# Four cost terms in a list scheduler's model: the port that VectorE and GpSimd share, transfer arrivals, block-solve matmuls, tile-size stickiness

## The chip, the cores and the metric

The kernel runs on one core of one Trainium2 chip. The core has a matrix engine (TensorE, PE in the profile, with its weight loads as PEld), VectorE (DVE), ScalarE (ACT), GpSimd (POOL) and SyncE (SP), which here only issues transfers. Each engine executes its own list of instructions in order and waits for the others at semaphores. SBUF is the on-chip memory, PSUM holds TensorE's results. The metric is device time in microseconds of one launch, lower is better.

## What is computed

Two trunk layers (D = 1024) over 640 tokens, of which 128 are a prompt and 512 a sample that starts from cached states. Each layer projects its modulated, normalised input to four recurrent mixers, each run forward and backward over the tokens, and has a feed-forward of 4096:

```python
def mixing_block(u, lp, init, pos):
    pa, pb, pc, pd = split_cols((u @ lp['w_in']), GROUP_COLS)
    ...  # mLSTM from pa, gated DeltaNet from pb, retention from pc, RWKV-7 from pd
    y = jnp.concatenate([ya, yb, yc, yd], axis=2).reshape(bsz, t, D_MODEL)
    return y @ lp['w_out'], (c1, n1, m1, sb1, sc1, sd1)

def trunk_layer(h, mod, lp, init, pos):
    sh1, sc1, g1, sh2, sc2, g2 = jnp.split(mod, 6, axis=-1)
    y, states = mixing_block(layer_norm(h) * (1.0 + sc1) + sh1, lp, init, pos)
    h = layer_norm(DEEPNORM_ALPHA * h + g1 * y, lp['ln1_g'], lp['ln1_b'])
    u = layer_norm(h) * (1.0 + sc2) + sh2
    f = jnp.square(jax.nn.relu(u @ lp['w_ff1'])) @ lp['w_ff2']
    h = layer_norm(DEEPNORM_ALPHA * h + g2 * f, lp['ln2_g'], lp['ln2_b'])
    return h, states
```

Here `mod = silu(cond) @ w_mod[l] + b_mod[l]`. Outputs are both token groups and the prompt's final states.

## The kernel before

The program is written once as plain calls, but nothing is issued then. Every call on an engine goes through `Engine.__getattr__` to `Plan.record`, which makes a node with its operands, its predecessors and an estimated duration from `Plan.cost` (for TensorE from `pe_time` and `pe_parts`). About 17,250 nodes come about. `Plan.schedule` then plays a run with these estimates: whenever an engine is free in that play, it takes the ready node of highest priority (`nd.prio`: place in the program, plus a little for the length of what follows) whose tiles can be had. `emit` issues the nodes in the order of their planned starts, so each engine's list, and SyncE's queue of transfers, is what the play produced. A different estimate thus changes the order of the lists, and nothing of what is computed. All instructions carry line 691 in the profile, the call in `emit`; the names of their tiles tell them apart.

Four things in the play matter here. First, the engine of some operations is chosen in it: `copyA` may run on ScalarE or VectorE, `tt` on VectorE or GpSimd, and a node moves off its preferred engine when the other is better by more than a slack. Second, TensorE's `pe_queue` prefers nodes of the tile size that runs already (128x128, or the small tiles of the block solves), unless another's priority is higher by `HY`. Third, a transfer's end is played as the later of a fixed latency and of the queue's bandwidth. Fourth, VectorE and GpSimd are played as independent.

Names used below. Full-precision products are made of a high and a low half: `split` takes a raw weight `wr` of 128x1024, `wh` is its rounded copy (`copyA`) and `wl` the difference (`tt`, GpSimd preferred); features have `uh` and `ul`, made from `u`. `pj` is a projection to a mixer, `pgj` that of the gates, `pwo` the output projection, `pff` the feed-forward. The modulation is made in chunks of 512 columns (`mod_chunk`): four products `pmod` from weights `wr` of `w_mod`, a copy `msb` to SBUF, in the gate sections the bias row by a transfer from `b_mod` into `msb`, then `pmt`, a second copy, and `pmg`, which puts the result into `modT`. `put` transposes a normalised tile `xn` before `u` is taken from it. In RWKV-7, `cum` are running sums of the log decay, `alp` and `kap` scaled keys, `psc` the score product of them, `lv` the 32x32 products of the block solves. `wscr` is a scratch in DRAM by which the solves' blocks are rearranged, `gh` what comes back from it.

The stages by the trace: start 0 to 120, mixing of layer 0 to 700, output projection and layer norm to about 790, its feed-forward to 1200, layer norm to 1300, mixing of layer 1 to 1850, output projection to 1937, feed-forward to 2347, and the end.

Of the kernel before, what the change touches and what calls it, by code (L numbers as in the profile page):

```python
# [80 lines left out]
class View:  # L81
    def __init__(self, tile, ops, p, ix, reg=None):
        self.tile, self.ops, self.p, self.ix, self.reg = tile, ops, p, ix, reg
# [130 lines left out]
class Plan:  # L214
    def __init__(self):
        self.nodes, self.tiles = [], []
        self.HY = 4.0
        self.bias = 0.0
        self.fill = False
        self.open_group, self.group_node = False, None  # L220
# [7 lines left out]
    @staticmethod  # L228
    def pe_parts(m, a):
        n = Plan.free_size(a[0])  # L230
        w = a[1].shape[1]
        w = 32 if w <= 32 else 64 if w <= 64 else 128
        if m == "transpose":
            return (n / 1200 + 0.0025,)
        if a[2].tile.dt == F32R:
            return (n / 2400 + 0.0135,)
        return (max(w / 1200, 2 * n / 2400) + 0.005,) * 2

    @staticmethod
    def pe_time(mem):  # L240
        t, end, pos = 0.0, 0.0, {}
        for m, fn, a, k in mem:
            p = (a[1].p[0], a[0].p[0])
            for d in Plan.pe_parts(m, a):
                t = max(t, pos.get(p, 0.0))
                pos[p] = t + d
                end = max(end, t + d)
                t += 0.0065
        return end
# [94 lines left out]
    def cost(self, nd, m, out, ins):  # L344
        e = nd.eng
        if e == "SP":
            o = nd.k["out"]
            i = nd.k["in_"]
            v = o if isinstance(o, View) else i
            n = 1  # L350
            for s in v.shape:
                n *= s
            return n * 4
        n = self.free_size(out)
        psum = any(v.tile.kind == "psum" for v in ins + [out])
        cols = sum(1 for v in ins if v.shape[-1] == 1 and n > 1)
        if e == "PE":
            return self.pe_time([(m, None, nd.a, nd.k)])
        if e == "DVE":
            if m in ("bn_stats", "reciprocal"):  # L360
                n = self.free_size(ins[0])
            if m == "bn_aggr":
                return 0.075
            if m in ("bn_stats", "transpose", "tensor_tensor_scan", "copy_predicated", "select", "tensor_tensor", "scalar_tensor_tensor") or psum:
                return n / 960 + 0.069 + (0.06 * cols if m != "tensor_scalar" else 0.0)
            return n / (1920 if m == "tensor_copy" else 1600) + 0.069 + 0.06 * max(0, cols - 1)
        if e == "ACT":
            return n / 1200 + (0.052 if psum else 0.094) + 0.093 * cols
        if e == "POOL":
            if m == "memset":  # L370
                return n / 1200 + 0.035
            if nd.k.get("op") == ALU.pow:
                return 0.165 * n + 0.3
            if m == "tensor_tensor":
                return n * 0.0021 + 0.148
            return n * 0.00333 + 0.176
        raise ValueError(e)
# [5 lines left out]
    def lat(self, a, b):  # L383
        if a == "SP":
            return 0.2 + SPM
        return self.LAT.get((a, b), 0.25)

    SPI = 0.48
    DLAT = 2.2
    DBW = 345.0*1e3  # L390

    def schedule(self):
        N = self.nodes
# [5 lines left out]
        for nd in reversed(N):  # L399
            d = nd.dur if nd.eng != "SP" else self.DLAT + nd.dur / self.DBW  # L400
            nd.cp = d + (max((self.lat(nd.eng, s.eng) + s.cp for s in nd.succs), default=0.0))
# [35 lines left out]
        for k, l in order.items():  # L437
            l.sort(key=lambda t: t.seq)
        nexti = dict.fromkeys(order, 0)
        for k, l in load.items():  # L440
            if l.max() > caps[k]:
                raise RuntimeError(f"{k} needs {l.max()} of {caps[k]}")
# [12 lines left out]
        free = {e: 0.0 for e in engs}  # L455
# [5 lines left out]
        dma_free = 0.0  # L461
# [3 lines left out]
        now = 0.0  # L465
# [89 lines left out]
        while True:  # L555
            progress = True
            while progress:
                progress = False
                for e in engs:
# [13 lines left out]
                    while h or e == "PE":  # L573
# [3 lines left out]
                        _, _, nd = heapq.heappop(q)  # L577
# [17 lines left out]
                        if b is not None:  # L595
                            wait[nd.idx] = nd
                            if b[0] == "g":
                                p = b[1]
# [19 lines left out]
                        if e == "PE":  # L618
                            cur = nd.grp
                            d = nd.dur + (SW if nd.mode != mode else 0.0)  # L620
                            mode = nd.mode
                            d *= 1 if warm else 2
                            hist.append((now, now + d, nd.act))
                            recent += nd.act
                            t0 = now
                            while t0 < now + d - 1e-9:
                                k = int(t0 / TICK + 1e-9)
                                t1 = min(now + d, (k + 1) * TICK)
                                cols[k] = cols.get(k, 0.0) + nd.act * (t1 - t0) / d
                                t0 = t1  # L630
                            nd.end = free[e] = now + d
                        elif e == "SP":
                            s = max(dma_free, now + 0.9)
                            dma_free = s + nd.dur / self.DBW
                            nd.end = max(now + self.DLAT, dma_free + 0.8)
                            free[e] = now + self.SPI
                        else:
                            nd.end = now + nd.dur
                            free[e] = nd.end
                        out.append(nd)  # L640
                        done += 1
# [24 lines left out]
            now = max(now, ev[0][0])  # L666
            while ev and ev[0][0] <= now + 1e-9:
                _, _, k, x = heapq.heappop(ev)
# [10 lines left out]
        if done != len(N):  # L679
            nd = N[floor]  # L680
# [1730 lines left out]
```

## Time and profile before

| | us |
|---|---|
| median of 3 runs | 2410.84 (2407.18 to 2411.10) |
| the profiled execution | 2401.18 |
| its span | 2399.5 |
| TensorE busy | 2125.6 (89%) |
| VectorE busy | 1536.5 (64%) |
| ScalarE busy | 937.9 (39%) |
| GpSimd busy | 702.4 (29%) |

The mean granted clock of TensorE was 0.929 in the profiled execution. A stage is read by setting the busy time of an engine against the stage's length; what ended an idle time is in the timeline's brackets.

### The profile page before, as it was taken

The page shows a single profiled execution, that of the slowest core. Times are in us where ns is not written, and L with a number is a line of the kernel's source. Part 1 is how long each engine was busy: PE and PEld are TensorE (multiplying, and loading weights), DVE is VectorE, ACT ScalarE, POOL GpSimd, SP SyncE. Part 2 cuts the span into 40 slices and gives each one's busy share as a digit, 9 for nine tenths or more (in the row PEclk, how much of TensorE's full clock was granted, in tenths as well). Part 3 has the DMA queues.
Part 4 walks back from the last instruction along what each step waited for, and adds up shares of the span by engine and source line. Part 5 has one row for each costly group of instructions (what it writes and reads, how often), then busy time and mean ns, then how long its engine had stood idle before and what let it go on. Part 6 is the DMA issues. An engine that isn't in the chain of part 4 may idle for free.

```text
span 2399.5 us, 42207 instructions
## 1 busy us (share of the span) xinstructions
PE 2125.6 (89%) x16510; PEld 1873.6 (78%) x16510; DVE 1536.5 (64%) x3349; ACT 937.9 (39%) x1979; POOL 702.4 (29%) x631
## 2 busy tenths in 40 slices
PE   5898798888887999999977898998988799999996
PEld 2787777687765988898866887888877689999994
DVE  5653965858679556655777758668976843333357
ACT  3332434333335544443334343343432443333332
POOL 2220512424047333333344313224423610000023
PEclk8978989899997999999998899899998899999998
DMA  8122324343644444444532121224245412222242
GB/s 262 28 65 74 81 82 132 76 118 87 207 141 150 126 124 138 140 132 123 177 107 63 36 68 36 64 75 102 82 127 168 140 62 79 71 79 78 72 158 88
DMA packets 317451, 253.13 MB, mean 105 GB/s; under 512 B 91100, under 2 KB 240828, under 8 KB 317252
## 3 DMA queue, kind: packets, MB, share of 16 engines
q1 hardware_dynamic: 317252, 250.43, 36.0%
q8 instruction: 130, 2.13, 0.4%
q14 instruction: 69, 0.57, 0.1%
HBM read 226.14 MB, written 24.24 MB: 104 GB/s over the span
## 4 chain that ended last, share of the span: by engine, by line
PE 32%; DVE 14%; issue 3%; DMA 2%; POOL 2%; ACT 1%; SPq 1%; POOLq 0%; ACTq 0%; DVEq 0%
PE pj L691 16%; PE pff L691 10%; DVE xn L691 2%; PE lv L691 1%; DVE cv L691 1%; DMA wr<-in_w_mod 1%; DVE acc L691 1%; DVE lnst L691 1%; DVE wl L691 1%; DVE osum L691 1%; PE poo L691 1%; SPq L691 1%; PE pwo L691 1%; DVE ew L691 0%; DVE fft L691 0%
## 5 line engine op out<-in xcount | busy, mean ns | idle before, releaser
L691 ACT CAST wh<-wr 128x1024 fp32r<-128x1024 f32 x228 | 238.8, 1048 | 453.4 <-PE pff L691 203.5
L691 PE MATMUL pff<-wh,hid 128*128 128x512 f32 x1280 | 403.2, 394 | 0.0
L691 PE MATMUL pj<-uh,wh 128*128 128x384 f32 (+1 forms) x1056 | 350.1, 332 | 9.3 <-ACT wh L691 8.5
L691 DVE TENSOR_TENSOR wl<-wr,wh 128x1024 fp32r<-128x1024 f32 x159 | 209.6, 1318 | 227.5 <-ACT wh L691 227.1
L691 PE MATMUL pj<-uh,wl 128*128 128x384 f32 (+1 forms) x1056 | 345.9, 329 | 9.2 <-POOL wl L691 5.3
L691 PE MATMUL pj<-ul,wh 128*128 128x384 f32 (+1 forms) x1056 | 343.8, 326 | 0.4 <-DVE ul L691 0.4
L691 PE MATMUL pj<-vh,wl 128*128 128x256 f32 (+1 forms) x1024 | 321.4, 314 | 6.5 <-POOL wl L691 5.5
L691 PE MATMUL pj<-vl,wh 128*128 128x256 f32 (+1 forms) x1024 | 320.9, 313 | 0.7 <-DVE vl L691 0.7
L691 PE MATMUL pj<-vh,wh 128*128 128x256 f32 (+1 forms) x1024 | 321.1, 314 | 0.3 <-ACT wh L691 0.3
L691 POOL TENSOR_TENSOR wl<-wr,wh 128x1024 fp32r<-128x1024 f32 x75 | 187.9, 2506 | 422.6 <-ACT wh L691 332.8
L691 PEld LDWEIGHTS pff<-wh,hid 128*128 128x128 f32 x1280 | 242.0, 189 | 51.3 <-issue 1.0
L691 PE MATMUL pff<-wl,hid 128*128 128x512 f32 x640 | 253.4, 396 | 11.2 <-POOL wl L691 8.5
L691 PEld LDWEIGHTS pj<-uh,wh 128*128 128x128 f32 x1056 | 210.7, 200 | 23.7 <-ACT wh L691 11.1
L691 PEld LDWEIGHTS pj<-uh,wl 128*128 128x128 f32 x1056 | 209.5, 199 | 16.4 <-POOL wl L691 7.0
L691 PEld LDWEIGHTS pj<-ul,wh 128*128 128x128 f32 x1056 | 209.8, 199 | 4.1 <-issue 0.8
L691 PEld LDWEIGHTS pj<-vh,wl 128*128 128x128 f32 x1024 | 197.4, 193 | 9.1 <-POOL wl L691 6.2
L691 PEld LDWEIGHTS pj<-vl,wh 128*128 128x128 f32 x1024 | 197.4, 193 | 2.3 <-POOL vl L691 0.9
L691 PEld LDWEIGHTS pj<-vh,wh 128*128 128x128 f32 x1024 | 197.3, 193 | 2.1 <-ACT wh L691 0.6
L691 POOL TENSOR_TENSOR mac<-mac,mtm 128x512 f32<-128x512 f32 x63 | 101.4, 1610 | 208.9 <-ACT mtm L691 179.5
L691 PEld LDWEIGHTS pff<-wl,hid 128*128 128x128 f32 x640 | 121.1, 189 | 41.7 <-POOL wl L691 10.6
L691 DVE SCALAR_TENSOR_TENSOR mac<-wr,cc,mac 128x512 f32<-128x512 f32 x84 | 87.5, 1042 | 90.9 <-DMA wr<-in_w_mod 81.3
L691 DVE TENSOR_TENSOR hid<-sqr,hid 128x256 fp32r<-128x256 f32 (+1 forms) x128 | 66.0, 521 | 124.2 <-ACT hid L691 124.0
(487 smaller groups left out, 3996.9 us busy)
## 6 DMA issues: line engine op xcount, KB each, us to landing
wr<-in_w_ff SPq DMA_DIRECT2D x136, 512.0 KB
wr<-in_w_mod SPq DMA_DIRECT2D x96, 512.0 KB
wr<-in_w_in SPq DMA_DIRECT2D x66, 512.0 KB
wr<-in_w_out SPq DMA_DIRECT2D x32, 512.0 KB
dq<-rscr SPq DMA_DIRECT2D x20, 256.0 KB
dec<-rscr SPq DMA_DIRECT2D x16, 320.0 KB
x1d<-x SPq DMA_DIRECT2D x20, 256.0 KB
xr<-x1d SPq DMA_DIRECT2D x20, 256.0 KB
```

Source lines behind the costliest of these rows:

```text
L691: fn(*[res(v) for v in a], **{k_: res(v) for k_, v in k.items()})
```

## The change

Four edits in `Plan`. `HY` goes from 4.0 to 1.0. In `pe_parts` a product with up to 32 columns on both sides costs 0.0103 us for each of its two passes, and in `pe_time` such products no longer run beside each other at different positions. A transfer with runs under 512 bytes costs proportionally more; a transfer begins 1.0 us after its issue, ends 1.2 us after the queue is through with it, and the queue moves 290 instead of 345 KB in a microsecond. And an operation of VectorE whose operands are all in SBUF is lengthened by half of its overlap with GpSimd, one of GpSimd by a fifth, with half of GpSimd's overlap handed on to VectorE's next such operation as `debt`.

```diff
-        self.HY = 4.0
+        self.HY = 1.0
...
+        if w == 32 and n <= 32:
+            return (0.0103,) * 2
         return (max(w / 1200, 2 * n / 2400) + 0.005,) * 2
...
-            p = (a[1].p[0], a[0].p[0])
+            p = (a[1].p[0], a[0].p[0]) if a[1].shape[1] > 32 or Plan.free_size(a[0]) > 32 else 0
...
-            return n * 4
+            run = min(x.shape[-1] * 4 for x in (o, i) if isinstance(x, View))
+            return n * 4 * max(1.0, 512 / max(4, run))
...
+    SHARED = ("tensor_tensor", "scalar_tensor_tensor", "tensor_copy", "tensor_scalar", "tensor_tensor_scan", "copy_predicated", "copy", "activation")
+    SHV, SHP = 0.5, 0.2
+
+    def shares(self, nd):
+        if nd.nm not in self.SHARED:
+            return False
+        return all(v.tile.kind == "sbuf" for v in list(nd.a) + list(nd.k.values()) if isinstance(v, View))
+
     SPI = 0.48
-    DLAT = 2.2
-    DBW = 345.0*1e3
+    DIN, DOUT = 1.0, 1.2
+    DLAT = DIN + DOUT
+    DBW = 290e3
...
+        vbusy, debt = 0.0, 0.0
...
                         elif e == "SP":
-                            s = max(dma_free, now + 0.9)
+                            s = max(dma_free, now + self.DIN)
                             dma_free = s + nd.dur / self.DBW
-                            nd.end = max(now + self.DLAT, dma_free + 0.8)
+                            nd.end = dma_free + self.DOUT
                             free[e] = now + self.SPI
                         else:
-                            nd.end = now + nd.dur
+                            d = nd.dur
+                            if e == "DVE" and self.shares(nd):
+                                d += debt
+                                debt = 0.0
+                                d += self.SHV * min(d / self.SHV, max(0.0, free["POOL"] - now))
+                                vbusy = now + d
+                            elif e == "POOL":
+                                o = min(d, max(0.0, vbusy - now))
+                                d += self.SHP * o
+                                debt += self.SHV * o
+                            nd.end = now + d
                             free[e] = nd.end
```

Counted over the whole program, 142 operations go from VectorE to GpSimd and 85 back, 134 from VectorE to ScalarE and 116 back. Of the low halves 147 instead of 159 stand on VectorE, 89 instead of 77 on GpSimd. TensorE changes its tile size 431 instead of 422 times. Its list is the same in the feed-forward of layer 1 and nearly the same in that of layer 0; in the mixing stages it is permuted.

Three places of the lists follow. A tile's name is followed by a running number, which differs between the two programs.

TensorE at the start, before, from the second part of the chunk `pmod_283` to the first transpose:

```order
L691 MATMUL pmod_283<-wr_194,cc 32x512 x2
L691 MATMUL pmt_298<-msb_288,cst 32x128 x4
L691 MATMUL pmod_283<-wr_196,cc 32x512 x2
L691 MATMUL pmod_283<-wr_214,cc 32x512 x2
L691 MATMUL pmg_308<-cst,msb_288 128x128
L691 MATMUL pmod_312<-wr_218,cc 32x512 x2
L691 MATMUL pmod_312<-wr_239,cc 32x512 x2
L691 MATMUL pmt_324<-msb_317,cst 32x128 x4
L691 MATMUL pmod_312<-wr_280,cc 32x512 x2
L691 MATMUL pmod_312<-wr_241,cc 32x512 x2
L691 MATMUL pmg_344<-cst,msb_317 128x128
L691 MATMUL put_348<-cst,xn_159 128x128
```

And now, from the sixth transpose on (five `put` rows and, before them, the `pmg_253` and `pmg_288` of the first two chunks are left out above):

```order
L714 MATMUL put_311<-cst,xn_243 128x128
L714 MATMUL put_324<-cst,xn_205 128x128
L714 MATMUL put_324<-cst,xn_243 128x128
L714 MATMUL put_333<-cst,xn_205 128x128
L714 MATMUL put_333<-cst,xn_243 128x128
L714 MATMUL put_342<-cst,xn_205 128x128
L714 MATMUL put_342<-cst,xn_243 128x128
L714 MATMUL put_350<-cst,xn_271 128x128
L714 MATMUL put_350<-cst,xn_290 128x128
L714 MATMUL put_357<-cst,xn_271 128x128
L714 MATMUL pmod_360<-wr_161,cc 32x512 x2
L714 MATMUL pmod_360<-wr_193,cc 32x512 x2
```

Transposes that need only the first two chunks stood behind the third and fourth; now 15 of them stand ahead of the third chunk's products. On ScalarE at the same place, before, the copies of the third and fourth chunk (`msb_317`, `msb_350`) among the high halves of the first weights:

```order
L691 COPY msb_317<-pmod_283 128x512
L691 CAST wh_320<-wr_310 128x1024
L691 COPY msb_317<-pmt_324 128x128
L691 CAST wh_338<-wr_329 128x1024
L691 CAST wh_342<-wr_331 128x1024
L691 COPY msb_350<-pmod_312 128x512
```

Now (third chunk `msb_387`, fourth `msb_416`):

```order
L714 COPY msb_387<-pmod_360 128x512
L714 CAST wh_389<-wr_385 128x1024
L714 COPY msb_387<-pmt_391 128x128
L714 CAST wh_407<-wr_396 128x1024
L714 COPY msb_416<-pmod_380 128x512
L714 ACTIVATE u_119_421<-put_357,modT_265 128x256
L714 CAST wh_435<-wr_405 128x1024
L714 COPY msb_416<-pmt_430 128x128
```

The first copy of the fourth chunk moved ahead of the third high half.

SyncE's queue around the bias row of a modulation chunk of layer 0 (near 598 us), before:

```order
L691 DMA wr_6480<-in_w_mod 128x2x512
L691 DMA wr_6490<-in_w_mod 128x2x512
L691 DMA wscr_1020_6546<-ew_6282 40x512
L691 DMA wscr_1020_6550<-ew_6282 40x512
L691 DMA wscr_1020_6546<-ei_5487 40x512
L691 DMA wscr_1020_6550<-ei_5487 40x512
L691 DMA wr_6565<-in_w_in 128x8x128
L691 DMA msb_6555<-in_b_mod 1x512
L691 DMA wr_6569<-in_w_mod 128x2x512
L691 DMA gh_6571<-wscr_1020_6546 128x10x32
L691 DMA gh_6571<-wscr_1020_6550 128x10x32
```

Now:

```order
L714 DMA wr_6351<-in_w_mod 128x2x512
L714 DMA wr_6414<-in_w_mod 128x2x512
L714 DMA wr_6516<-in_w_in 128x8x128
L714 DMA wr_6526<-in_w_mod 128x2x512
L714 DMA msb_6520<-in_b_mod 1x512
L714 DMA wscr_1020_6574<-ew_6319 40x512
L714 DMA wscr_1020_6576<-ew_6319 40x512
L714 DMA wr_6578<-in_w_mod 128x2x512
L714 DMA wscr_1020_6574<-ei_5477 40x512
L714 DMA wscr_1020_6576<-ei_5477 40x512
L714 DMA wr_6584<-in_w_in 128x8x128
```

The bias row `msb` stands ahead of the four stores to `wscr`, where it stood behind them; two weights moved ahead of them as well. On TensorE, the `pmt` that needs it moved behind 19 rows of the next weight's projection.

VectorE in the mixing of layer 1 (near 1342 us), around the `kap` of the one direction, before:

```order
L691 SCALAR_TENSOR_TENSOR cum_13091<-tw_13562,cst 128x128
L691 TENSOR_TENSOR kts_13573<-kts_13573,dk_13474 128x640
L691 SCALAR_TENSOR_TENSOR cum_13091<-tw_13562,cst 128x128 x4
L691 SCALAR_TENSOR_TENSOR alp_13601<-ta_13578,dk_13474 128x640
L691 SCALAR_TENSOR_TENSOR alp_13564<-alp_13564,dcol_10644,wm_13594 128x640
L691 SCALAR_TENSOR_TENSOR kap_13616<-dk_13474,pcol_7974,cum_12969 128x640
L691 COPY e_2340_13622<-cum_12969 128x5
L691 TENSOR_TENSOR wm_13594<-kts_13573,wm_13594 128x640
```

Now:

```order
L714 SCALAR_TENSOR_TENSOR cum_13093<-tw_13561,cst 128x128
L714 TENSOR_TENSOR kts_13571<-kts_13571,dk_13482 128x640
L714 SCALAR_TENSOR_TENSOR cum_13093<-tw_13561,cst 128x128 x2
L714 SCALAR_TENSOR_TENSOR alp_13564<-alp_13564,dcol_10651,wm_13584 128x640
L714 SCALAR_TENSOR_TENSOR cum_13093<-tw_13561,cst 128x128
L714 SCALAR_TENSOR_TENSOR kap_13598<-dk_13482,pcol_7996,cum_12979 128x640
L714 COPY e_2340_13606<-cum_12979 128x5
L714 SCALAR_TENSOR_TENSOR cum_13093<-tw_13561,cst 128x128
L714 TENSOR_TENSOR g_2341_13611<-e_2340_13606,e_2338_13573 128x4
L714 COPY cmid_13613<-cum_13093 128x5
L714 SCALAR_TENSOR_TENSOR alp_13616<-ta_13579,dk_13482 128x640
L714 TENSOR_SCALAR ta_13579<-ta_13579,dcol_10651 128x640
```

The first `alp` of the other direction, `alp_13601` before and `alp_13616` now, moved behind `kap`, and so did one of the `cum` scans.

## Rows read from the trace of the kernel before

**Rows 1.** Busy time of each engine over the whole span, from the page's first part.
```profile
PE 2125.6 (89%) x16510; PEld 1873.6 (78%) x16510; DVE 1536.5 (64%) x3349; ACT 937.9 (39%) x1979; POOL 702.4 (29%) x631
```

**Rows 2.** Stages: length; busy PE, PEld, DVE, ACT, POOL (x instructions); clock; DMA share, GB/s.
```profile
0.00:120.00 120.00, 82.05 (x499) 61.08 (x501) 70.47 (x188) 44.36 (x100) 31.81 (x43) 0.88 0.46 145
120.00:700.00 580.00, 501.21 (x5139) 434.44 (x5138) 370.09 (x1069) 208.77 (x522) 157.34 (x163) 0.90 0.39 105
700.00:790.00 90.00, 71.03 (x323) 58.51 (x322) 84.66 (x130) 46.19 (x81) 64.56 (x54) 0.83 0.44 136
780.00:1200.00 420.00, 409.53 (x2410) 365.85 (x2409) 258.48 (x322) 191.36 (x338) 143.58 (x81) 0.98 0.45 137
1300.00:1850.00 550.00, 493.08 (x5153) 451.00 (x5153) 407.89 (x1156) 218.75 (x551) 171.05 (x174) 0.94 0.31 80
1937.00:2347.00 410.00, 410.00 (x2333) 375.45 (x2333) 155.18 (x199) 147.77 (x255) 15.30 (x10) 1.00 0.28 85
```

**Rows 3.** Waits of TensorE by releaser: us in all, times, longest us.
```profile
PE psc L691 <- DVE kap L691: 15.7, 3, 7.7
...
PE pj L691 <- POOL wl L691: 10.8, 6, 4.3
...
PE pmt L691 <- DMA msb<-in_b_mod: 9.2, 2, 6.5
...
PE pff L691 <- POOL wl L691: 8.5, 5, 3.0
...
PE pwo L691 <- POOL wl L691: 8.0, 5, 3.4
...
PE lv L691 <- issue: 7.1, 7, 1.9
```

**Rows 4.** Timeline of the start, TensorE, ScalarE, VectorE: start, us, operation, [idle before <- releaser].
```profile
31.64 1.07 PE L691 MATMUL pmod<-wr,cc 128*32 128x512 f32 x2 [6.31 <-DMA wr<-in_w_mod]
...
49.91 0.48 PE L691 MATMUL pmg<-cst,msb 128*128 128x128 f32 x1 [1.80 <-ACT msb L691]
...
50.18 4.93 PE L691 MATMUL put<-cst,xn 128*128 128x128 f32 x29
...
45.04 1.04 ACT L691 CAST wh<-wr 128x1024 fp32r<-128x1024 f32 x1 [0.67 <-DMA wr<-in_w_in]
...
46.00 0.58 ACT L691 COPY msb<-pmod 128x512 f32<-128x512 f32 x1
...
49.60 0.26 ACT L691 COPY msb<-pmt 128x128 f32<-128x128 f32 x1
...
60.46 0.76 DVE L691 TENSOR_TENSOR ul<-u,uh 128x256 fp32r<-128x256 f32 x2
```

**Rows 5.** Timeline of SyncE's queue and of TensorE from 596 to 602.
```profile
596.77 0.65 SPq L691 DMA_DIRECT2D wscr<-ei  x2
...
598.00 0.47 SPq L691 DMA_DIRECT2D msb<-in_b_mod  x1
...
601.68 0.66 PE L691 MATMUL pmt<-msb,cst 128*32 128x128 f32 x8 [6.46 <-DMA msb<-in_b_mod]
```

**Rows 6.** Timeline of VectorE and TensorE around one kap of layer 1.
```profile
1342.31 1.97 DVE L691 SCALAR_TENSOR_TENSOR alp<-ta,dk 128x640 f32<-128x640 f32 x1
...
1345.92 2.51 PE L691 MATMUL psc<-kap,alp 64*128 64x128 f32 x20 [5.01 <-DVE kap L691]
```

**Rows 7.** Groups of low halves by engine: count, busy us, mean ns, idle before.
```profile
L691 DVE TENSOR_TENSOR wl<-wr,wh 128x1024 fp32r<-128x1024 f32 x159 | 209.6, 1318 | 227.5 <-ACT wh L691 227.1
...
L691 POOL TENSOR_TENSOR wl<-wr,wh 128x1024 fp32r<-128x1024 f32 x75 | 187.9, 2506 | 422.6 <-ACT wh L691 332.8
```

**Rows 8.** Timeline of VectorE and of GpSimd in the last stage.
```profile
2354.44 1.28 DVE L691 TENSOR_TENSOR acc<-acc,fft 128x512 f32<-128x512 f32 x2
...
2356.84 2.38 DVE L691 TENSOR_TENSOR acc<-acc,fft 128x512 f32<-128x512 f32 x1
...
2356.26 2.42 POOL L691 TENSOR_TENSOR wl<-wr,wh 128x1024 fp32r<-128x1024 f32 x1 [32.00 <-ACT wh L691]
```

## The prediction, made before the changed kernel was run

> **What bounds the kernel now.** I read the busy shares first: TensorE 2125.6 us of the 2399.5 us span, VectorE 64%, GpSimd 29% [rows 1]. So TensorE is the bound, and only its idle time, 2399.5 − 2125.6 = 274 us, can be won by another order: the change alters no instruction of it. Next the table by stage [rows 2], where the reader should set TensorE's busy time against the length. The second feed-forward (1937 to 2347) has no idle time, the first (780 to 1200) 420 − 409.5 = 10.5 us, but the start 120 − 82.1 = 38, the two mixing stages 580 − 501.2 = 79 and 550 − 493.1 = 57, the stage of output projection and layer norm behind the first one 90 − 71 = 19. Then the waits of TensorE by their releaser [rows 3]: no single one is large. VectorE's kap gives 15.7 us, the bias row of the modulation 9.2, low halves of weights made by GpSimd 10.8 + 8.5 + 8.0. A better order can therefore win some ten or twenty microseconds here and there and no more; it can lose as much, since every wait is a neighbour of another one.
>
> The profiled execution took 2401.18 us, the median of the runs is 2410.84; I make the sum against 2401.18 and then take the difference from 2410.84.
>
> **The change part by part.** The plan's costs change, so the change is what its lists become. The two lists were set against each other instruction by instruction.
>
> Start. Before, TensorE stands 6.31 us at 31.64 for a weight of the third modulation chunk, while the transposes into features that need only the first two chunks are queued behind it; the last pmg stands at 49.91, and 29 of 40 transposes come after it [rows 4]. Their evacuation lasts until VectorE's 60.46 + 0.76 = 61.2, so 11.3 us for 29. Now 15 transposes stand ahead of that wait, 4 between, 20 of the 40 behind the last pmg: 9 fewer, 9/29 × 11.3 = 3.5 us. The other half is ScalarE: its copy of the last chunk (46.00) was queued behind a cast that began at 45.04 after waiting for its weight. Now it stands a cast earlier, and the second copy (49.60) right behind the cast of 45.04, which ends at 46.1: the last pmg moves from 49.91 to about 46.6, 3.3 us. I take **−7**. Least is −1, if the weights' transfers stretch (nothing behind them is earlier then); most −10, if the earlier first features also free VectorE.
>
> Bias row. At 601.68 TensorE waits 6.46 us for the bias of a modulation chunk. SyncE issued that transfer at 598.00, behind four stores of wscr, the last pair of which waited until 596.77 for ScalarE's copy [rows 5]. Now the bias is ahead of the stores, and the product that needs it 19 matmul rows behind the next weight's projection. That wait goes whole if the projection's weight has its buffer when the list asks for it, else the wait moves to that weight, which before was issued between the stores and the bias. With the second wait of this kind (9.2 − 6.46 = 2.7 [rows 3]) the ends are −9 and −3; I take **−6.5**, since the wait was at the head of SyncE's queue and not in a buffer.
>
> Block of kap. VectorE ran 1.97 us of alp for the other direction just before the kap that TensorE stood 5.01 us for [rows 6]; now that alp stands behind it, with one of four scans, so some 2.3 us of the wait go. The same swap is made at the longest of the three waits in layer 0 (7.7 of the 15.7 us [rows 3]), where about as much goes. **−5**, between 0 (the other direction's psc then waits for alp) and −8.
>
> Low halves. TensorE stood 27.3 us for low halves of GpSimd [rows 3]. One takes 2.506 us there and 1.318 on VectorE [rows 7], a difference of 1.19. Of halves that TensorE waits for or nearly, 7 go from GpSimd to VectorE (−8.3 at most) and 9 the other way; those cost 1.19 each if they start when they did, but GpSimd stands idle before most, so half a microsecond each: +4.5. **−4**, between −8 and +4.
>
> Projection matmuls put ahead of other waits. Beside kap and the bias, the mixing stages idle 79 + 57 − 15.7 − 9.2 = 111 us. In the new list about 60 us of these waits have projection matmuls moved ahead of them that are as long as the wait. But the projection is one fixed pool of work, and a matmul moved to one hole leaves another. I credit a fifth, **−12**; the ends are 0 (all give it back) and −36 (three fifths stay).
>
> New waits. At the end of the second mixing stage 4 to 6 us of VectorE's work now stands ahead of Rd, Yd and osum of the last head; one high half of a weight at 767 stands behind a ScalarE row that waits; in 334 to 360 a chain is put later. I take **+9**, between 0 and +20. Less weight on staying in a tile size adds 9 switches (422 to 431). The nearest row is the wait without releaser ahead of the small solves: 7.1 us in 7, so at most 1.0 each, mostly hidden behind the weight load: **+1**, between 0 and +9.
>
> GpSimd. It gets 142 operations from VectorE and gives 85 back, at their durations before +92 us for it and −67 for VectorE. GpSimd is busy 29% [rows 1], so it carries this outside the stages of layer norm. But operations of the two that read two operands in SBUF get in each other's way: two additions of acc take 1.28 us together, while a third beside a GpSimd low half (2356.26, 2.42 us) takes 2.38 and ends behind it [rows 8]: 1.7 us lost. If each of the 57 added operations met one of VectorE, that were 57 × 1.7 = 97 us; VectorE is busy 64% of the time, and I estimate that half of its work reads SBUF twice, so 97 × 0.64 × 0.5 = 31, less than the 67 it is rid of, and most of either lies beside TensorE's work. I count **0**, with +15, half of the 31, as the end. The Trainium skill, SBUF — State Buffer, section Who interferes with whom, calls the pair of ports an exclusive lock for which the loser fully blocks; rows 8 agree with it. By that rule every overlap is lost whole by one of the two, this line would be +15, and the median 2401.
>
> Sum: −7 − 6.5 − 5 − 4 − 12 + 9 + 1 = −24.5, so 2401.18 becomes 2376.7, and the median about **2386**.
>
> **The rivals.** *The waits only change place.* Each item above hands its time to the next dependence, since mixing stages are chains of small operations, in which TensorE, VectorE and transfers alternate. For it: the waits are many and short, none of those in rows 3 but kap over 11 us in all. Against: bias and start are waits at the head of a queue, not in a chain. The start alone stays: −4, 2407; between 2402 and 2415.
>
> *Slower: GpSimd becomes the engine waited for.* Where VectorE is nearly full, in 700 to 790 (84.7 of 90 us, GpSimd 64.6 [rows 2]) and its like behind layer 1, what it loses to GpSimd it can't make up. There GpSimd gets 28 us more, some 11 low halves at 2.5 us; each blocks one VectorE operation for 1.7 us (+19) and is 1.19 us later for TensorE (+13), and half of the start's gain remains: about +25 against a remaining −10, 2426. It decides if more than about half of these 11 are waited for. Against: the low halves have no more than a few tenths of slack in the list, and it would have to hold in stages that the plan saw as full.
>
> *More than forecast.* Three fifths of the covered waits stay gone: −24 more, 2362.
>
> *The lists differ and the time doesn't follow the model at all*: layer 1's feed-forward is unchanged in order, so 17% of the span can't move; that is in the sums.
>
> **How the numbers follow.** Forecast (2374 to 2400) 0.50, more 0.12, waits change place 0.21, slower 0.17. Something like ±0.2% (±4.8 us) is what a measurement of this kernel tells from no change: faster is below 2406.0, slower above 2415.7. Of "change place" a bit under a third lies below 2406, and a fifth of it above 2415.7, so faster 0.50 + 0.12 + 0.06 = 0.68, less 0.04 for a forecast that misses upward, 0.64; same 0.15; slower 0.21. For 8 in 10: the low end goes to "more", 2362; the high end into the slower case, whose middle is 2426: 2420.
>
> **What would show it.** Right: the last pmg of the start near 46.6 (49.91 now), no wait of over 3 us at the product of the modulation's bias, kap under 11 us in all, TensorE's idle time from 274 to about 250. TensorE's busy time stays within 5 us of 2125.6, or its clock moved instead. Wrong: TensorE waiting over 40 us for GpSimd's low halves (27.3 now), or VectorE's SBUF additions longer on average; then the slower rival. If the waits named are gone and idle time is the same 274, the first rival.

## Result and profile after

The changed kernel took 2384.76 us (median of 4 runs, 2375.1 to 2393.0) against 2410.41 of before: a ratio of 0.9895, 95% interval 0.9852 to 0.9937. The forecast was 2386. Its profiled execution took 2389.08 us with a span of 2387.3, 12 us less than that of before: of the two profiles the one of before is faster than its kernel's median, and the one of after slower.

The busy time of each engine (answers to [rows 1]):

```profile
PE 2131.1 (89%) x16510; PEld 1883.6 (79%) x16510; DVE 1547.2 (65%) x3274; ACT 942.6 (39%) x1997; POOL 769.8 (32%) x688
```

TensorE's idle time is 2387.3 − 2131.1 = 256 us, where it was 274; its busy time is 5.5 us longer. Stretches as in [rows 2], after; columns as there:

```profile
0.00:120.00 120.00, 91.36 (x564) 71.00 (x565) 74.87 (x195) 47.38 (x109) 35.76 (x49) 0.93 0.48 147
120.00:700.00 580.00, 509.28 (x5167) 437.24 (x5166) 394.04 (x1083) 211.21 (x524) 176.62 (x179) 0.91 0.40 112
...
1300.00:1850.00 550.00, 491.10 (x4951) 445.40 (x4950) 387.94 (x1076) 202.76 (x517) 193.86 (x182) 0.88 0.32 80
```

Since the changed kernel runs ahead, fixed stretches no longer hold the same work. Between program marks (first projection, middle product of the output projection, first and last feed-forward product), worked out from the instructions' times and the records of the granted clock in the two traces, the table is as follows (a mixing stage has 5507 products of TensorE in layer 0 and 5327 in layer 1, the first feed-forward 2486, in both programs):

| us in the stage (of it at 1.2 GHz) | before | after |
|---|---|---|
| start, to the first projection | 55.6 (24) | 52.2 (14) |
| mixing 0, to the middle of the output projection | 647.7 (116) | 623.8 (102) |
| from there to the first feed-forward product | 93.9 (31) | 97.8 (27) |
| feed-forward 0 | 451.4 (14) | 437.2 (5) |
| to the first projection of layer 1 | 21.5 (19) | 23.4 (23) |
| mixing 1, to the middle of the output projection | 597.1 (87) | 623.9 (142) |
| from there to the first feed-forward product | 90.2 (27) | 86.7 (17) |
| feed-forward 1 | 421.8 (1) | 423.7 (3) |

So the reader sees three large movements and not one: −24 in mixing 0, −14 in feed-forward 0, and +27 in mixing 1. By the same marks TensorE's idle time fell from 89.3 to 70.5 us in mixing 0 and from 16.0 to 7.4 in feed-forward 0; the rest of the gain is busy time, 5 and 6 us, with 14 and 9 us less at 1.2 GHz. In mixing 1 idle time is nearly the same (66.5 and 69.6), and the same products take 24 us more, with 55 us more at the lower clock.

Waits of TensorE by releaser, answers to [rows 3]:

```profile
PE lv L714 <- issue: 15.1, 12, 3.7
...
PE pff L714 <- POOL wl L714: 10.3, 6, 3.7
...
PE psc L714 <- DVE e L714: 6.5, 1, 6.5
PE pwo L714 <- POOL wl L714: 6.1, 7, 1.5
PE pmt L714 <- ACT msb L714: 6.0, 3, 2.9
...
PE pj L714 <- POOL wl L714: 3.5, 4, 1.6
...
PE psc L714 <- DVE kap L714: 2.9, 2, 2.5
```

kap fell from 15.7 to 2.9, GpSimd's low halves from 27.3 to 10.3 + 6.1 + 3.5 = 19.9, the bias row's transfer is gone; the wait ahead of the solves' products went up from 7.1 to 15.1. The 6.5 us for `e` stand at the place of [rows 6], where 5.01 for kap stood. VectorE's kap there before; then scan and kap of after with GpSimd's `wm`, and TensorE's product:

```profile
1345.00 0.87 DVE L691 SCALAR_TENSOR_TENSOR kap<-dk,pcol,cum 128x640 f32<-128x640 f32 x1
```

```profile
1308.53 1.63 DVE L714 TENSOR_TENSOR_SCAN cum<-tw,cst 128x128 f32<-128x128 f32 x1
1309.83 1.64 POOL L714 TENSOR_TENSOR wm<-kts,wm 128x640 f32<-128x640 f32 x1
1310.07 2.08 DVE L714 SCALAR_TENSOR_TENSOR kap<-dk,pcol,cum 128x640 f32<-128x640 f32 x1
```

```profile
1312.30 2.51 PE L714 MATMUL psc<-kap,alp 64*128 64x128 f32 x20 [6.46 <-DVE e L714]
```

`alp` is behind kap, as planned, but kap took 2.08 us and not 0.87: `wm`, which VectorE did behind it before, runs on GpSimd beside it now, and kap ends 0.7 us behind `wm`, as the addition of [rows 8] did behind its neighbour. The scan took 1.63 us beside GpSimd's `rho` (1308.34 to 1309.87), where four took 1.36 before. So VectorE's way from the first `kts` product to the end of kap is no shorter (4.8 us before, 5.0 now), while TensorE comes to its wait 1.2 us sooner.

The start, TensorE, then ScalarE, answers to [rows 4]:

```profile
27.51 3.41 PE L714 MATMUL put<-cst,xn 128*128 128x128 f32 x15
30.84 1.97 PE L714 MATMUL pmod<-wr,cc 128*32 128x512 f32 x8
...
48.07 0.47 PE L714 MATMUL pmg<-cst,msb 128*128 128x128 f32 x1 [0.51 <-ACT msb L714]
48.34 4.06 PE L714 MATMUL put<-cst,xn 128*128 128x128 f32 x20
52.15 0.42 PE L714 MATMUL pj<-uh,wh 128*128 128x384 f32 x1
```

```profile
44.92 1.04 ACT L714 CAST wh<-wr 128x1024 fp32r<-128x1024 f32 x1 [1.59 <-DMA wr<-in_w_in]
45.87 0.58 ACT L714 COPY msb<-pmod 128x512 f32<-128x512 f32 x1
...
46.81 1.04 ACT L714 CAST wh<-wr 128x1024 fp32r<-128x1024 f32 x1
47.75 0.27 ACT L714 COPY msb<-pmt 128x128 f32<-128x128 f32 x1
```

15 transposes run at 27.51, ahead of the third chunk's products, which now wait for nothing at 30.84; 20 are left behind the last pmg. That pmg came at 48.07 and not at 46.6, because ScalarE's copies of the last chunk stand between casts that came later: the second cast began at 44.92, after 1.59 us for its weight, and the third at 46.81, where the third of before began at 45.04 [rows 4].

The bias row of layer 0, SyncE's queue, then TensorE, answers to [rows 5]:

```profile
565.39 0.26 SPq L714 DMA_DIRECT2D msb<-in_b_mod  x1
574.32 0.67 SPq L714 DMA_DIRECT2D wscr<-ew  x2
...
575.54 0.79 SPq L714 DMA_DIRECT2D wscr<-ei  x2
```

```profile
576.89 0.43 PE L714 MATMUL pmt<-msb,cst 128*32 128x128 f32 x8
```

It was issued 9 us ahead of the stores, and its product at 576.89 has no idle time before it.

### The profile page after: what moved, and what is told of

Same layout as the page of the kernel before. It is cut to its first block, busy times and chain, and to the rows that moved or that the text cites. A ratio compares the mean times of both kernels' runs of the same rounds, so it can differ in the third digit from the quotient of the medians.

```text
span 2387.3 us, 42205 instructions
## 1 busy us (share of the span) xinstructions
PE 2131.1 (89%) x16510; PEld 1883.6 (79%) x16510; DVE 1547.2 (65%) x3274; ACT 942.6 (39%) x1997; POOL 769.8 (32%) x688
## 4 chain that ended last, share of the span: by engine, by line
PE 59%; DVE 20%; DMA 7%; POOL 5%; issue 5%; ACT 3%; SPq 1%; POOLq 0%; ACTq 0%; DVEq 0%
PE pj L714 29%; PE pff L714 16%; DVE xn L714 2%; DMA wr<-in_w_mod 2%; PE lv L714 2%; DMA wr<-in_w_in 2%; PE pwo L714 2%; PE poo L714 1%; DVE osum L714 1%; POOL wl L714 1%; DVE cv L714 1%; DVE lnst L714 1%; PE pzz L714 1%; POOL hrs L714 1%; DVE acc L714 1%
## 5 line engine op out<-in xcount | busy, mean ns | idle before, releaser
L714 ACT CAST wh<-wr 128x1024 fp32r<-128x1024 f32 x233 | 244.2, 1049 | 480.8 <-PE pff L714 241.2
L714 PE MATMUL pj<-uh,wh 128*128 128x256 f32 (+1 forms) x1056 | 349.1, 331 | 5.9 <-ACT wh L714 3.8
L714 PE MATMUL pj<-uh,wl 128*128 128x256 f32 (+1 forms) x1056 | 342.4, 326 | 4.4 <-POOL wl L714 3.5
L714 DVE TENSOR_TENSOR wl<-wr,wh 128x1024 fp32r<-128x1024 f32 x147 | 190.0, 1293 | 237.9 <-ACT wh L714 237.6
L714 POOL TENSOR_TENSOR wl<-wr,wh 128x1024 fp32r<-128x1024 f32 x87 | 216.9, 2494 | 281.9 <-ACT wh L714 250.9
L714 PE MATMUL pff<-wl,hid 128*128 128x512 f32 x640 | 253.7, 396 | 10.3 <-POOL wl L714 10.3
L714 POOL TENSOR_TENSOR mac<-mac,mtm 128x512 f32<-128x512 f32 x77 | 117.7, 1529 | 204.7 <-ACT mtm L714 185.5
L714 DVE TENSOR_TENSOR hid<-sqr,hid 128x256 fp32r<-128x256 f32 (+1 forms) x123 | 73.0, 595 | 121.0 <-ACT hid L714 120.7
L714 POOL TENSOR_TENSOR acc<-acc,bc 128x512 f32<-128x512 f32 x15 | 23.9, 1604 | 379.5 <-DVE acc L714 378.3
```

The source lines that it names most:

```text
L714: fn(*[res(v) for v in a], **{k_: res(v) for k_, v in k.items()})
```

## Experiments

Each run was set beside the kernel before on the same chip; ratios are of medians with 95% intervals. The kernel before had there 2400.7 us (the four edits alone), 2399.9 (the next four runs) and 2402.9 (the last four), which is why times are compared by their ratios. The question was which of the four edits carries the change, whether a change of lists without meaning would do as much, and where the time went.

**The transfer model alone.** Kernel before with only this part of the change:

```diff
-            return n * 4
+            run = min(x.shape[-1] * 4 for x in (o, i) if isinstance(x, View))
+            return n * 4 * max(1.0, 512 / max(4, run))
...
+    DIN, DOUT = 1.0, 1.2
+    DBW = 290e3
...
+                            s = max(dma_free, now + self.DIN)
+                            nd.end = dma_free + self.DOUT
```

> Kernel before with only the transfer model of the change (DIN, DOUT, 290 KB in a microsecond, short runs dearer). Theory A (named waits at the heads of queues): this edit alone puts 15 transposes ahead of the third modulation chunk, so the first gate projection moves from 55.6 to about 52.5 and the bias wait of 6.5 us goes; median 2400, at most 2404. Theory B (any other order would give as much, the edits' content doesn't matter): start 3 us earlier but the total anywhere between 2395 and 2425. Theory C (the gain is the port's model): 2407, only the start.

Measured: 2369.68 us, ratio 0.9884 (0.9851 to 0.9916), the whole gain and more than theory A gave it. Theory C falls. The start moved (first projection 53.0), and so did the waits for weights. TensorE's waits between 60 and 640 of before, and then of this run:

```profile
PE pj L691 <- ACT wh L691: 8.5, 6, 3.5
...
PE pmt L691 <- DMA msb<-in_b_mod: 6.5, 1, 6.5
...
PE pj L691 <- POOL wl L691: 5.3, 4, 2.3
...
PE pmod L691 <- DMA wr<-in_w_mod: 2.5, 1, 2.5
```

```profile
PE pmod L693 <- DMA wr<-in_w_mod: 8.7, 4, 3.1
...
PE pj L693 <- ACT wh L693: 2.6, 2, 1.4
...
PE pj L693 <- POOL wl L693: 1.3, 2, 1.0
...
PE pmt L693 <- DMA msb<-in_b_mod: 0.4, 1, 0.4
```

Of 8.5 + 6.5 + 5.3 = 20.3 us for the projection's weights and the bias, 2.6 + 1.3 + 0.4 = 4.3 are left; the modulation's own products give 6.2 of the difference back (2.5 to 8.7). Mixing 0 took 616.9 us, 31 less than before, with 71.4 us of TensorE idle (89.3 before) and 68 us at 1.2 GHz (116 before).

**The shared port alone.** Kernel before with `SHARED`, `shares`, `SHV`, `SHP` and the branch that uses them.

> Kernel before with only the port shared by VectorE and GpSimd in the model. Its list gives GpSimd 73 operations more. Theory A: low halves and VectorE's chains gain, 2402, with TensorE's waits for GpSimd's low halves not over 30 us in all. Theory C: it carries most of the gain, 2392. Rival of the prediction (GpSimd becomes the engine waited for): 2420 or more, with over 40 us of waits for low halves.

Measured: 2405.85, ratio 1.0021 (0.9998 to 1.0044). GpSimd got 786 us of work where it had 702, and TensorE's waits for its low halves are under those of before:

```profile
PE pff L710 <- POOL wl L710: 11.4, 7, 3.7
...
PE pwo L710 <- POOL wl L710: 6.0, 6, 1.5
PE pj L710 <- POOL wl L710: 5.5, 5, 2.9
```

22.9 us in all against 27.3. So the model of the port moves the work, and that is worth nothing in the total; nor did GpSimd become the engine waited for. This edit by itself already gives the changed kernel's waits at kap (3.0 us for kap, 6.7 for `e`); with the transfer model alone kap is at 10.1.

**Less stickiness alone**: `HY` 4.0 to 1.0 on the kernel before.

> Kernel before with only HY 4.0 to 1.0. Its list changes tile size 436 instead of 421 times. Theory A: nothing but a microsecond of switches, 2408 to 2413. If the stickiness held up chains in the mixing stages: 2400 or less.

Measured: 2411.36, ratio 1.0054 (1.0029 to 1.0078): slower by half a percent. The wait ahead of the solves' products, by which I priced a switch of tile size, hardly rose with 15 switches more:

```profile
PE lv L691 <- issue: 7.9, 6, 2.2
```

**Block-solve durations alone**: the two lines in `pe_parts` and `pe_time` on the kernel before.

> Kernel before with only the durations of block-solve products changed (32 by 32 products one after the other). Theory A: waits of the solves (lv) shift by a few microseconds, 2405 to 2413. Theory B: anywhere between 2395 and 2425.

Measured: 2415.23, ratio 1.0074 (1.0048 to 1.0101), above what I gave it. That wait doubled, with 2 switches more:

```profile
PE lv L693 <- issue: 15.3, 11, 3.3
```

So the 15.1 us of the changed kernel belong to the block-solve costs and not to switches.

**All but the transfer model**: the changed kernel with the four lines of the transfer model as before.

> Changed kernel with the transfer model of before (port, stickiness and block-solve costs as changed). Theory A, sharpened by the four edits run alone (only the transfer model gained, 1.2%): the gain goes, 2405 to 2420, start again with the first projection near 55.6. Theory D (the four edits work together and no single one carries the change): about 2390.

Measured: 2425.05, ratio 1.0097 (1.0063 to 1.013). Without the transfer model the three other edits make the kernel one percent slower. Theory D falls.

**Noise on the lists.** A change without meaning, on the kernel before with two seeds, and on the transfer model alone:

```diff
     def schedule(self):
         N = self.nodes
+        rnd = np.random.default_rng(1)
...
             nd.preds = list(nd.preds.values())
+            if nd.eng == "PE":
+                nd.dur *= 1 + 0.02 * (2 * rnd.random() - 1)
```

> Kernel before in which the scheduler sees TensorE's durations with a random 2% up or down (first seed), a change without meaning that permutes the lists about as much as the block-solve edit. Theory A: within 0.5% of before on either side, 2395 to 2415. Theory B (any reshuffle gives as much): may be 1% faster, 2375, or 1% slower.

> The same noise with another seed on the kernel before. Theory A: 2395 to 2415. Theory B: spread of 1% over the seeds, so that one in two or three is under 2385.

> Kernel before with the transfer model of the change alone, and the same random 2% on TensorE's durations. Theory A (the transfer model's content carries the gain): 2365 to 2385 again. Theory B (the list that came out was a lucky one): it falls back to 2395 or more.

Measured: 2409.29, ratio 1.0026 (1.0003 to 1.0048); 2402.25, ratio 1.0006 (0.9981 to 1.0031); and with the transfer model 2371.48, ratio 0.9857 (0.9814 to 0.99). A reshuffle without meaning is worth up to 0.3% here (two seeds), and the gain of the transfer model survives one. Theory B falls: of the lists without that model, none is faster than before (1.0006 to 1.0097).

**Which part of the transfer model.** Without the dearer short runs, and then with the latency only (DIN and DOUT, the bandwidth left at 345):

> Kernel before with latency and bandwidth of the transfer model as changed, but short runs not dearer. Theory E (weights are played as arriving later, so lists stop putting their consumers at the head of ScalarE, VectorE and TensorE too early): the waits of ScalarE and VectorE for in_w_mod between 60 and 1200 fall from 220 us (99 + 40 + 81) to about 100 as in the run with the whole transfer model, feed-forward 0 is 10 us shorter, 2375 to 2385. The start is as before, since the list has no transposes ahead of the third chunk without the dearer short runs: first projection 55.6. Rival F (short runs carry the gain): 2395 or more and those waits stay near 220 us.

> Kernel before with only DIN and DOUT in place of 0.9, 0.8 and the fixed latency; bandwidth 345 and short runs as before. A 512 KB weight is played as landing 0.5 us later than before, where the whole edit makes it 0.8. Theory E: about 0.5/0.8 of the effect, waits for in_w_mod about 145 us, 2380 to 2390. Rival G (bandwidth is what counts, since the queue backs up): no change, 2400.

Measured: 2378.02, ratio 0.9901 (0.9877 to 0.9925), with the first projection at 55.6 as expected; and 2404.78, ratio 1.001 (0.9983 to 1.0037). Rival F falls. With the latency alone theory E was wrong in size: it gave 2380 to 2390 and nothing came, so rival G (the bandwidth counts) holds for that step. Bandwidth without latency was not run, and the bandwidth also enters `nd.prio`, by the length of what follows, which this run leaves as before; the two ways were not told apart.

**Later still**: the transfer model alone with `DOUT` 2.4.

> The whole transfer model with DOUT 2.4 instead of 1.2, so every landing is played 1.2 us later again. Theory E: waits for in_w_mod fall further, under 60 us, and the time is level or a little better, 2360 to 2375, as long as buffers allow earlier issues; small dependent transfers are then overrated, so a few microseconds in the mixing stages may go back. Rival H (the numbers of the edit fit the chip, any more is as wrong as less): 2390 or more.

Measured: 2370.69, ratio 0.9852 (0.9824 to 0.9879), the fastest of this set, below the changed kernel beside it (0.9909). Rival H falls: more than the edit's numbers does no harm. That it helps is not shown, since the transfer model as it is has 0.9884 and 0.9857.

**The changed kernel again.**

> The changed kernel once more, beside the kernel before of these runs: ratio 0.985 to 0.995, so 2370 to 2388. With the transfer model alone at 0.988 and 0.986, the other three edits are worth nothing or cost up to 0.5%. The half-clock time of the mixing of layer 1 (153 us in the first profile, 92 in that of before) shows whether that was one execution's or the list's: over 130 again if it is the list.

Measured: 2380.37, ratio 0.9909 (0.9885 to 0.9934). The expectation's 153 and 92 us are taken from a stretch 11 us too early; by the marks they are the 142 and 87 of the table above. Taken in the same way this execution has 135, over the 130, and by the marks 124, with mixing 1 at 616.2 us: the slower clock is for the most part the list's, and some of it that execution's.

**Where the transfer model acts.** A weight of 512 KB on an empty queue is played as usable 0.9 + 1.5 + 0.8 + 0.2 = 3.4 us after its issue in before (0.2 is the play's way from queue to engine), 3.9 with the latency only, 4.2 with the whole model, 5.4 with landings later still. In the trace of before TensorE, ScalarE or VectorE waited for such a weight 106 times; it released them 3.5 us after its issue at the least, in the median 4.3. So before plays, on an empty queue, every one of these too early.

In feed-forward 0 the weights of layer 1's modulation are multiplied on ScalarE and VectorE (`mac`, `mtm`) between the feed-forward's own steps. Waits from 785 to 1225 of ScalarE and VectorE for these weights, before:

```profile
ACT mtm L691 <- DMA wr<-in_w_mod: 99.3, 31, 6.7
ACT mac L691 <- DMA wr<-in_w_mod: 39.8, 9, 7.0
...
DVE mac L691 <- DMA wr<-in_w_mod: 81.3, 31, 4.9
```

The changed kernel, and then the run with the transfer model alone:

```profile
ACT mtm L714 <- DMA wr<-in_w_mod: 40.2, 23, 7.1
ACT mac L714 <- DMA wr<-in_w_mod: 7.9, 4, 2.8
...
DVE mac L714 <- DMA wr<-in_w_mod: 30.7, 20, 3.9
```

```profile
ACT mtm L693 <- DMA wr<-in_w_mod: 48.6, 23, 6.4
ACT mac L693 <- DMA wr<-in_w_mod: 11.1, 6, 3.1
...
DVE mac L693 <- DMA wr<-in_w_mod: 32.2, 17, 3.7
```

In before the two engines stood 99.3 + 39.8 + 81.3 = 220 us for a weight at the head of their lists; what the feed-forward and the modulation wanted of them stood behind. All runs of this study, by these waits (rounded) and by the length of feed-forward 0:

| run | waits for in_w_mod, us | feed-forward 0, us |
|---|---|---|
| stickiness alone | 228 | 449.3 |
| before | 220 | 451.4 |
| block solves alone | 220 | 446.7 |
| before with noise 1, 3 | 215, 207 | 447.9, 448.7 |
| port alone | 203 | 456.0 |
| all but the transfer model | 190 | 445.5 |
| latency only | 182 | 445.3 |
| transfer model alone, with noise | 92, 108 | 440.8, 439.0 |
| without short runs | 101 | 436.6 |
| the change, twice | 79, 76 | 437.2, 437.4 |
| later still | 46 | 433.5 |

All eight runs above 180 us have 445 to 456, all six at or below 108 have 433 to 441. Within either group the order is loose. No run changes these waits by themselves, so that they shorten the stage is argued from the two groups. Mixing 0 parts them less well: 617 to 625 us in the lists with the model but 640 with landings later still, 639 to 670 in those without. In feed-forward 0 TensorE itself stood for ScalarE's copies of the modulation (`pmg`), 5.6 us before and 1.7 in the changed kernel:

```profile
PE pmg L691 <- ACT msb L691: 5.6, 3, 3.1
```

```profile
PE pmg L714 <- ACT msb L714: 1.7, 1, 1.7
```

**The clock in mixing 1.** Stretches of the changed kernel's first trace, columns as in [rows 2], then the waits of TensorE just before:

```profile
1470.00:1480.00 10.00, 10.00 (x48) 9.78 (x45) 5.28 (x25) 2.81 (x12) 2.46 (x6) 0.50 0.27 51
1480.00:1490.00 10.00, 10.00 (x49) 8.19 (x48) 5.46 (x25) 4.00 (x7) 4.21 (x4) 0.50 0.21 54
1490.00:1500.00 10.00, 10.00 (x55) 8.96 (x52) 4.83 (x15) 0.88 (x3) 1.18 (x5) 0.55 0.01 3
1500.00:1510.00 10.00, 10.00 (x90) 9.14 (x88) 9.29 (x33) 4.93 (x9) 0.00 (x0) 1.00 0.05 16
```

```profile
1466.53 0.48 PE L714 MATMUL psc<-kap,alp 64*128 64x128 f32 x2 [1.90 <-ACT tk L714]
1469.04 1.65 PE L714 MATMUL psc<-kap,alp 64*128 64x128 f32 x10 [2.02 <-DVE dq L714]
```

At 0.50 to 0.55, the lower of the clock's two levels (1.2 GHz), TensorE is busy for all of 30 us; it had stood 1.90 and 2.02 us in the 6 us before, and its work in the stretch is products of up to 130 columns among projections. In [rows 2] the mean clock of 1300 to 1850 was 0.94, in the changed kernel 0.88, and 0.90 in its second trace:

```profile
1300.00:1850.00 550.00, 488.35 (x4989) 441.91 (x4990) 393.64 (x1081) 204.74 (x520) 195.73 (x183) 0.90 0.32 81
```

By the table TensorE spent 142 − 87 = 55 us more at the lower level; its busy time for the same products is 24 us longer and its idle time 3 us, which makes the 27. It does not come with the transfer model as such: of the four lists with that model, whole or in part, and without the other edits, one has 135 us at 1.2 GHz in mixing 1 (the model alone), three have 83 to 91 (with noise, without short runs, later still), and their mixing 1 takes 613 and 593 to 598 us.

## Why the prediction came out right, and which steps did not

The time was right (2386 against 2384.8), on a sum whose terms were right in part, and in part by luck. The sum was made against the profile of before, 2401.18 − 24.5; the profile of after is 12.1 us shorter and not 24.5, and the medians agree because the two profiles lie on different sides of theirs (in the last set the medians part by 22.6 us). The step ahead of all terms, that only TensorE's idle time can be won, does not hold: the same 16,510 products take from 2106.9 us (the model with noise) to 2136.4 (all but the model) of busy time. Of the signs named, busy time moved by 5.5 us, over the 5 that were to mean a moved clock; idle time is 256 for about 250. Taken by steps:

- **Start, −7.** The mechanism held, the size was off: the first projection came 3.4 us earlier. The step that failed is the 3.3 us for ScalarE: I let the casts begin when they had, and they began 1.6 to 1.8 us later. That the reorder needs the dearer short runs is shown: without them the first projection is at 55.6 again.
- **Bias row, −6.5.** Right: its waits of 9.2 us are gone. Of the 6.0 us for ScalarE's copy 2.9 stand in mixing 0, at 341.8, the others at the start, where 1.9 us for VectorE stood; the net in mixing 0 is −6.3.
- **Block of kap, −5.** Right in the number, half right in the mechanism. In layer 0 the wait went from 7.7 to 2.5. At the place of [rows 6] it went from 5.01 to 6.46, since kap and the scan, beside GpSimd, lost what the swap had won, and TensorE came sooner; I had named the other direction's psc as the price. All waits of psc together went from 20.4 to 16.2 us.
- **Low halves, −4.** Right in sign, 27.3 to 19.9, and TensorE's waits for VectorE's low halves, which I had not read, went from 13.9 to 4.2. But the port's edit alone saves 4.4 of the 27.3 and the total does not move, so this term should not have been counted in full.
- **Projection matmuls ahead of waits, −12, and new waits, +9.** This was the weak step. I spread a guess over both mixing stages. Mixing 0 gained 24 us, bias and kap included, 19 of them in idle time (with the transfer model alone the waits for the projection's weights and the bias went from 20.3 to 4.3 us); mixing 1 lost 27. The loss came as a lower clock and not as waits, and no term of the sum had the clock in it.
- **Switches, +1.** The named row did rise, by 8 us, near the bound of +9, but for another reason: the block-solve edit alone does it, and 15 switches more don't.
- **Feed-forward 0.** I counted it at nothing since TensorE's order hardly changes there. It gained 14 us, 9 of them idle time of TensorE: the waits of ScalarE's and VectorE's `mac` and `mtm` fell, and I had read only TensorE's list. The 220 us of waits of these two engines were in the trace of before, and I had read no waits but TensorE's.
- **GpSimd, 0.** Right: 67 us more work on it, and ratio 1.0021 for that edit by itself. The rival of the exclusive lock gave +15, or 0.6%, and that edit's interval ends at 0.44%. The Trainium skill, SBUF — State Buffer, section Who interferes with whom, says that the one that comes second fully blocks; [rows 8] and the kap of 2.08 us agree, but in the total neither its cost nor the gain of playing it could be measured.

So two terms that were left out, −14 in feed-forward 0 and +27 of clock in mixing 1, were offset in part by a mixing 0 that gained more than I credited. What is shown: the transfer model carries the gain (0.9884, 0.9857 with noise), the others together cost 1.0% without it. Whether they cost anything beside it is not settled: 0.9909 (0.9885 to 0.9934) with them and 0.9884 (0.9851 to 0.9916) without, from different sets of runs. Why the lists with a low clock in mixing 1 have it stays open too; idle time there does not tell them apart (64.1 us in the model alone, 63.8 with noise, at 135 and 83 us of lower clock).

## What to carry to other kernels

In this scheduler's model the times at which data arrive were worth more than the other three edits: a consumer that is listed before its data have landed holds up all that stands behind it in its engine's list, while listing it later cost nothing here. Landings played 1.2 us later again, at 5.4 us where the median of the waits is 4.3, kept the gain. And an operation moved to another engine has to be checked against its new neighbour: kap lost by `wm` what the new order had won. When a model is changed in four ways at once, run each alone and add a noise control, and read the lists of every engine that waits, not only that of the bound one.

## What the runs showed of the hardware

TensorE can spend 30 us at the lower of its two clock levels while it is busy throughout (0.50 to 0.55 from 1470 to 1500), after gaps of no more than about 2 us (1.90 and 2.02). And of two lists with nearly the same idle time in mixing 1 (64.1 and 63.8 us) one spent 135 us at 1.2 GHz and the other 83, so idle time alone does not tell what the clock will do.

VectorE's kap (128x640, two operands in SBUF) takes 0.87 us by itself. Two of the eight in before take over 1.5 us, five in the changed kernel (up to 2.08) and one with the transfer model alone; each of these ends 0.7 us behind an operation of GpSimd that began before it, and a kap that began first keeps its 0.87. So work given to GpSimd cost VectorE here, though the total does not show it.

Of 106 waits for a 512 KB weight none ended sooner than 3.5 us after its issue; the median is 4.3, the longest 9.9.
